# Mixer B's values product in three rounded parts, with small operations moved to GpSimd

## The chip, the cores and the metric

The kernel runs on one core of one Trainium2 chip. A core has five engines that run their own instruction queues in order: TensorE (PE, matmuls and transposes into PSUM), VectorE (DVE), ScalarE (ACT), GpSimd (POOL) and SyncE (SP, which issues transfers). The metric is the device time of one execution, in microseconds; of several runs the median is told. A profiled execution gives the trace, from which the rows below come.

## The reference

A two-layer encoder trunk over 512 positions of width 1024, all in fp32. Layer 0 has a dilated window attention (mixer A), layer 1 a latent attention (mixer B); each is followed by a squared-ReLU MLP. What matters here is mixer B:

```python
lat = h @ w_in                                   # 256 q latents, 128 kv latents, 64 rotary key
q  = (rms_norm(c_q, q_a_gain) @ w_qb)            # 8 heads x (128 + 64)
kv = (rms_norm(c_kv, kv_a_gain) @ w_kvb)         # 8 heads x (128 keys + 128 values)
q, k = rms_norm(q, q_gain), rms_norm(k, k_gain)  # k = key part and the shared rotary key
# rope on the last 64 of q and k
p = softmax(q k^T / sqrt(192)); o = p v          # every position attends to every position
return o @ w_o
```

## The kernel before

The kernel is written as a program that a scheduler turns into one queue for each engine: it lists operations in program order and picks, by its own cost model, which ready operation goes next on its engine. So an edit in one place can move instructions of the same stretch on every engine. Tiles come from pools with a fixed number of buffers; a new tile in a used buffer waits for the last reader of the old one.

Almost all matmuls work on rounded parts: a value x is split into `hi` (x in the reduced fp32 format F32R, written by ScalarE) and `lo` (x - hi, written by VectorE), and a product is the sum of hi*hi, hi*lo and lo*hi. One product of mixer B is not: probabilities times values (`pv_b`, L1157) reads plain fp32 tiles.

Mixer B works as follows. The latents of four row blocks are projected (L1162) and normalised (`evac_lat`, L996): squares are summed on ScalarE, epsilon is added on VectorE, the power -0.5 is taken on GpSimd (both in `rstd_of`, L127), and VectorE scales. The rotary key is made by three products on VectorE and a sum on GpSimd. Heads go in four pairs. For a pair, `kv_chunk` projects one row block of keys and values (L1051), scales the keys (`ks`, L1105) and transposes them; `q_chunk` does the same for queries, with their rotary part in three products on VectorE (L1069, L1072) and a sum on GpSimd (L1076). Their PSUM tiles come from a pool of two banks.

Scores come next, one block of 128 queries of one head per step (`score`, L1125): five matmuls (L1133), the row maximum on VectorE (L1135), its product with the query's scale on VectorE (L1136), the exponential on ScalarE (L1138), the reciprocal of the sum (L1139) and the normalisation (L1140) on VectorE. Three steps later the block is transposed by TensorE and copied out of PSUM, even blocks by VectorE (L1151), odd ones by ScalarE (L1149). After the fourth block of a head comes the product with the values, `pv_b`, whose result is split into parts for the output projection (L1159, L1160). In the first three pairs scores, transposed blocks and outputs share a pool of four PSUM banks; in the last pair these four hold the output projection, whose matmuls run beside the scores.

The chunks of the next pair are laid between the steps by a table, `plan`: from the third step of a pair on, one or two chunks a step; the first two steps of a pair have none of the next pair. Weight blocks of the projections behind are also split in this stretch (L158 on ScalarE, L159 on VectorE).

Of the kernel before, what the change touches and what calls it, by code (L numbers as in the profile page):

```python
# [10 lines left out]
F32 = mybir.dt.float32  # L11
# [77 lines left out]
def encoder_kernel(ctx: ExitStack, tc: tile.TileContext, x, norm_mix, norm_ffn, a_w_qkv, a_q_gain, a_k_gain,  # L89
# [37 lines left out]
    def rstd_of(ss, n, add, name, out=None):  # L127

        v = st.tile([P, 8], F32, tag="rs_v", name=nm("rs_v"))
        V.tensor_scalar(v[:, :n], ss, add, None, op0=ALU.add)  # L130
        if out is None:
            out = st.tile([P, 8], F32, tag=name, name=nm(name))[:, :n]
        G.tensor_tensor(out, v[:, :n], nhalf[:, :n], op=ALU.pow)  # L133
        return out
# [835 lines left out]
    if True:  # L970
        with tc.tile_pool(name="bpool", bufs=1, reuse_waits="tile") as bp, \
# [10 lines left out]
            cgB = bp.tile([P, NT, 2, RD], F32, name="cgB")  # L982
            sgB = bp.tile([P, NT, 2, RD], F32, name="sgB")

            with tc.issue_after(marks["sum"]):
                for t in range(2):
                    for hf in range(2):
                        gb = gr[:, t, hf * 32:hf * 32 + 32].unsqueeze(1).broadcast_to([P, NT, 32])
                        G.tensor_tensor(cgB[:, :, t, hf * 32:hf * 32 + 32], cosB, gb, op=ALU.mult)
                        G.tensor_tensor(sgB[:, :, t, hf * 32:hf * 32 + 32], sinB, gb, op=ALU.mult)  # L990
                G.tensor_scalar(sgB[:, :, :, 32:64], sgB[:, :, :, 32:64], -1.0, None, op0=ALU.mult)
# [4 lines left out]
            def evac_lat(r, acc):  # L996
# [6 lines left out]
                rs = rstd_of(ss[:, 0:2], 2, EPS, "lrs")  # L1003
                cn = bw.tile([P, QL + KVL], F32, tag="cn", name=nm("cn"))
# [3 lines left out]
                t2 = bw.tile([P, 2 * RD], F32, tag="kr2", name=nm("kr2"), bufs=1)[:, 0:RD]  # L1008
# [17 lines left out]
            def new_pair(p):  # L1026
# [4 lines left out]
                d["v"] = bw.tile([P, NT, 2, DH], F32, tag="vb", name=nm("vb"), bufs=2)  # L1031
# [23 lines left out]
            def q_chunk(d, r):  # L1055
# [8 lines left out]
                rstd_of(ss[:, 0:2], 2, QKD * EPS, None, d["rq"][:, r])  # L1064
                qs = bw.tile([P, 2, DH], F32, tag="qs", name=nm("qs"), bufs=2)
                A.activation(qs, a3[:, :, 0:DH], AF.Copy)
                rt = bw.tile([P, 2, RD], F32, tag="rt", name=nm("rt"), bufs=1)
                r2 = bw.tile([P, 2, RD], F32, tag="r2", name=nm("r2"), bufs=1)
                V.tensor_tensor(rt, a3[:, :, DH:QKD], cgB[:, r, 0].unsqueeze(1).broadcast_to([P, 2, RD]), op=ALU.mult)  # L1069
# [176 lines left out]
```

## Time and profile before

| | |
|---|---|
| median of 3 runs | 1409.34 us (1408.19 to 1409.35) |
| the profiled execution | 1411.71 us, of which the span of the trace 1409.9 us |
| granted TensorE clock, mean | 0.999 |
| TensorE busy | 1374.4 us, 97% |
| VectorE busy | 940.8 us, 67% |
| ScalarE busy | 801.2 us, 57% |
| GpSimd busy | 225.3 us, 16% |

Shares are averages over stages with different limits. Matmuls are pipelined, so the busy time of one contains waiting; the distance from one matmul's start to the next tells more. The chain of waits follows the work that ended last back through the engines. An idle time in the timeline has, behind an arrow, what ended it.

### The profile page before, as it was taken

The numbers are of one execution on the slowest core, as the hardware profiler recorded it, in microseconds if no ns is written. First come the engines' busy times: TensorE is split into PE (matmuls) and PEld (weight loads), VectorE is DVE, ScalarE is ACT, GpSimd is POOL, SyncE is SP. The second block draws the span as 40 slices with busy tenths as digits, with TensorE's granted clock in tenths as the row PEclk, the third lists the DMA queues.
The fourth block names the chain that finished last, engine by engine and source line by source line (L and its number), as shares of the span: only waits on it lengthen the run. The fifth ranks groups of instructions, "written<-read, shape, count | busy, mean of one in ns | idle before, by whom it ended". The sixth has DMA issues, their size and how long they took to land.

```text
span 1409.9 us, 18981 instructions
## 1 busy us (share of the span) xinstructions
PE 1374.4 (97%) x6852; PEld 1165.1 (83%) x6852; DVE 940.8 (67%) x1498; ACT 801.2 (57%) x1643; POOL 225.3 (16%) x240
## 2 busy tenths in 40 slices
PE   7999999999999999999999999899999999999998
PEld 6999878888889979888888878776768888888886
DVE  6885777787788744574655768788644465574747
ACT  6544778687786624553536455777523553644543
POOL 1110212121122001020200204523101020020201
PEclk9999999999999999999999999999999999999999
DMA  9535554655555538586683934200114758493835
GB/s 304 167 134 160 134 133 98 164 130 126 143 131 119 155 105 244 159 187 172 124 234 91 234 90 94 60 30 31 45 45 165 194 125 233 92 236 121 197 87 120
DMA packets 171774, 197.83 MB, mean 140 GB/s; under 512 B 59104, under 2 KB 109024, under 8 KB 171680
## 3 DMA queue, kind: packets, MB, share of 16 engines
q1 hardware_dynamic: 152496, 157.55, 37.8%
q0 software_dynamic: 19184, 39.07, 15.4%
q8 instruction: 54, 0.88, 0.3%
q14 instruction: 40, 0.33, 0.1%
HBM read 176.13 MB, written 7.86 MB: 130 GB/s over the span
## 4 chain that ended last, share of the span: by engine, by line
PE 80%; DVE 7%; DMA 5%; ACT 5%; issue 2%; SPq 0%; POOL 0%; ACTq 0%; DVEq 0%; POOLq 0%
PE acc L183 45%; PE sc L860 11%; PE tp L860 7%; DMA xT<-t 3%; PE tp L125 3%; PE sc L422 2%; PE acc L1157 1%; PE sc L1051 1%; PE acc L1133 1%; PE tp L422 1%; DVE wlo L803 1%; PE acc L422 1%; PE sco L702 1%; ACT junk L138 1%; PE sc L588 1%
## 5 line engine op out<-in xcount | busy, mean ns | idle before, releaser
L183 PE MATMUL acc<-whi,hT 128*128 128x512 f32 (+2 forms) x1208 | 378.0, 389 | 1.9 <-ACT hT L744 1.0
L183 PE MATMUL acc<-hT_f,whi 128*128 128x512 f32 (+1 forms) x1152 | 316.6, 366 | 0.0
L159 DVE TENSOR_TENSOR wlo<-raw,whi 128x1024 fp32r<-128x1024 f32 (+3 forms) x146 | 173.1, 1189 | 162.4 <-ACT whi L158 161.8
L183 PEld LDWEIGHTS acc<-whi,hT 128*128 128x128 f32 x1208 | 225.0, 189 | 43.5 <-ACT hT L744 1.8
L158 ACT ACTIVATE whi<-raw 128x1024 fp32r<-128x1024 f32 (+3 forms) x146 | 149.9, 1029 | 160.6 <-PE acc L183 64.4
L183 PEld LDWEIGHTS acc<-hT_f,whi 128*128 128x128 f32 x1152 | 207.5, 189 | 34.7
L183 PE MATMUL acc<-wlo,hT 128*128 128x512 f32 (+2 forms) x604 | 233.5, 387 | 0.7 <-DVE wlo L159 0.7
L803 DVE TENSOR_TENSOR wlo<-wqs,whi 128x1024 fp32r<-128x1024 f32 x112 | 137.7, 1232 | 112.4 <-ACT whi L802 112.2
L802 ACT ACTIVATE whi<-wqs 128x1024 fp32r<-128x1024 f32 x112 | 118.3, 1060 | 160.5 <-PE acc L183 66.2
L183 PE MATMUL acc<-hT_f,wlo 128*128 128x512 f32 (+1 forms) x576 | 204.1, 365 | 0.0
L860 PE MATMUL sc<-whi,asp 128*128 128x512 f32 x512 | 165.0, 389 | 1.2 <-DVE resid L834 1.2
L788 POOL DMA_DIRECT2D wqs<-in_ffn_w_dram x64 | 77.6, 1344 | 536.8 <-DVE wlo L803 356.5
L183 PEld LDWEIGHTS acc<-wlo,hT 128*128 128x128 f32 x604 | 113.8, 189 | 20.4 <-DVE wlo L159 1.1
L183 PEld LDWEIGHTS acc<-hT_f,wlo 128*128 128x128 f32 x576 | 108.2, 189 | 17.5
L860 PEld LDWEIGHTS sc<-whi,asp 128*128 128x128 f32 x512 | 96.1, 188 | 21.8 <-issue 2.0
L860 PE MATMUL tp<-whi,asp 128*128 128x512 f32 x352 | 112.1, 389 | 0.9 <-DVE resid L834 0.9
L133 POOL TENSOR_TENSOR qrs<-rs_v,nhalf 128x4 f32<-128x4 f32 x48 | 65.9, 1375 | 264.6 <-DVE rs_v L130 233.7
L860 PE MATMUL sc<-wlo,asp 128*128 128x512 f32 x256 | 99.6, 389 | 0.0
L296 ACT ACTIVATE qkT<-xT 128x1024 uint16<-128x1024 uint16 x48 | 56.5, 1183 | 43.0 <-DMA xT<-t 42.8
L860 PEld LDWEIGHTS tp<-whi,asp 128*128 128x128 f32 x352 | 66.1, 188 | 15.0 <-DVE resid L834 1.3
L860 PE MATMUL tp<-wlo,asp 128*128 128x512 f32 x176 | 68.1, 389 | 0.0
L138 ACT ACTIVATE junk<-acc 128x128 f32<-128x128 f32 x192 | 52.2, 272 | 11.0 <-PE acc L183 7.3
(236 smaller groups left out, 2189.0 us busy)
## 6 DMA issues: line engine op xcount, KB each, us to landing
wqs<-in_ffn_w_dram SPq DMA_DIRECT2D x80, 512.0 KB, 5.6
raw<-in_ffn_w_dram SPq DMA_DIRECT2D x64, 512.0 KB, 4.4
wqs<-in_ffn_w_dram POOLq DMA_DIRECT2D x64, 512.0 KB, 7.9
raw<-in_a_w_qkv_dram SPq DMA_DIRECT2D x96, 256.0 KB, 3.2
b<-in_a_w_qkv_dram SPq DMA_DIRECT2D x24, 384.0 KB, 5.7
vall<-vo POOLq DMA_DIRECT2D x24, 192.0 KB, 2.3
raw<-in_a_w_o_dram SPq DMA_DIRECT2D x8, 512.0 KB, 4.2
raw<-in_b_w_o_dram SPq DMA_DIRECT2D x8, 512.0 KB, 3.8
```

Source lines behind the costliest of these rows:

```text
L125: return PE.transpose(o, i, ident)
L133: G.tensor_tensor(out, v[:, :n], nhalf[:, :n], op=ALU.pow)
L138: A.activation(junk, x, AF.Square, scale=1.0 / math.sqrt(dim), accum_out=out)
L158: A.activation(hi[:, :nk, :n], raw[:, :nk, :n], AF.Copy)
L159: V.tensor_tensor(lo[:, :nk, :n], raw[:, :nk, :n], hi[:, :nk, :n].bitcast(F32), op=ALU.subtract)
L183: PE.matmul(accs[o][:, oc], lhsT=lt, rhs=rt, start=(kt == 0 and p_i == 0 and hv == 0), stop=(kt == total - 1 and p_i == 2), skip_group_che ...
L296: A.activation(dst, xT.rearrange("p (h c) t -> p c t h", h=2), AF.Copy)
L422: PE.matmul(banks[t][:, :VH], lhsT=lt, rhs=rt[:, j], start=(first and k == 0 and i_ == 0), stop=(k == 3 and i_ == 2), skip_group_check=True)
L788: marks["sum"] = nc.gpsimd.dma_start(t, src, accum_op=ALU.add).ins
L802: A.activation(hi, x, AF.Copy)
L803: V.tensor_tensor(lo, x, hi.bitcast(F32), op=ALU.subtract)
L860: PE.matmul(bk[t], lhsT=lt, rhs=rt[:, j], start=(first and k == 0 and i_ == 0), stop=(k == 3 and i_ == 2), skip_group_check=True)
```

## The change

The product of probabilities and values is made of three products of rounded parts, like the others. The values get a rounded part and a remainder (`vl`, VectorE; for odd pairs in the buffer of the gain table), the transposed probabilities too: all 32 blocks are rounded by ScalarE, and VectorE writes all 32 remainders. One tile of parts serves all heads; before, two heads had a tile each. The sum with epsilon in the reciprocal roots of mixer B, and the scaling of a maximum, go from VectorE to GpSimd. The rotary products of a query chunk are one operation on VectorE instead of three, from a table `csB` in which cosines and sines stand together, and the sum on GpSimd is two operations; likewise for the rotary key. The normalised latents take a buffer of the probabilities' tag.

```diff
-    def rstd_of(ss, n, add, name, out=None):
+    def rstd_of(ss, n, add, name, out=None, on=None):
...
-        V.tensor_scalar(v[:, :n], ss, add, None, op0=ALU.add)
+        (on or V).tensor_scalar(v[:, :n], ss, add, None, op0=ALU.add)
...
-                V.tensor_tensor(krr[:, r], acc[:, 384:448], cgB[:, r, 1], op=ALU.mult)
-                V.tensor_tensor(t2[:, 0:32], acc[:, 416:448], sgB[:, r, 1, 32:64], op=ALU.mult)
-                V.tensor_tensor(t2[:, 32:64], acc[:, 384:416], sgB[:, r, 1, 0:32], op=ALU.mult)
-                G.tensor_tensor(krr[:, r], krr[:, r], t2, op=ALU.add)
+                V.tensor_tensor(t2, acc[:, 384:448].unsqueeze(1).broadcast_to([P, 2, RD]), csB[:, r, 1], op=ALU.mult)
+                for hf in range(2):
+                    o_ = 32 - 32 * hf
+                    G.tensor_tensor(krr[:, r, hf * 32:hf * 32 + 32], t2[:, 0, hf * 32:hf * 32 + 32],
+                                    t2[:, 1, o_:o_ + 32], op=ALU.add)
...
-                d["v"] = bw.tile([P, NT, 2, DH], F32, tag="vb", name=nm("vb"), bufs=2)
+                d["v"] = [bw.tile([P, NT, 2, DH], F32R, tag="vb", name=nm("vb"), bufs=2),
+                          gp.tile([P, NT, 2, DH], F32R, tag="gain", name=nm("vl")) if p % 2 else
+                          bw.tile([P, NT, 2, DH], F32R, tag="vl", name=nm("vl"), bufs=1)]
...
-                V.tensor_tensor(rt, a3[:, :, DH:QKD], cgB[:, r, 0].unsqueeze(1).broadcast_to([P, 2, RD]), op=ALU.mult)
+                V.tensor_tensor(rt, a3[:, :, DH:QKD].unsqueeze(1).broadcast_to([P, 2, 2, RD]),
+                                csB[:, r, 0].unsqueeze(2).broadcast_to([P, 2, 2, RD]), op=ALU.mult)
...
-                rs = rstd_of(ss[:, 0:2], 2, ssr[:, r:r + 1], "krs")
-                A.activation(d["v"][:, r], a4[:, :, 1], AF.Copy)
+                rs = rstd_of(ss[:, 0:2], 2, ssr[:, r:r + 1], "krs", on=G)
+                vh, vl = (t[:, r] for t in d["v"])
+                A.activation(vh, a4[:, :, 1], AF.Copy)
+                V.tensor_tensor(vl, a4[:, :, 1], vh.bitcast(F32), op=ALU.subtract)
...
-                V.tensor_scalar(mx[:, 1:2], mx[:, 0:1], rq, -1.0, op0=ALU.mult, op1=ALU.mult)
+                G.tensor_scalar(mx[:, 1:2], mx[:, 0:1], rq, -1.0, op0=ALU.mult, op1=ALU.mult)
...
-                    dst = pT[:, :, r * P:(r + 1) * P]
-                    if r % 2:
-                        A.activation(dst, tv, AF.Copy)
-                    else:
-                        V.tensor_copy(dst, tv)
+                    hi, lo = (pT[:, c, :, r * P:(r + 1) * P] for c in range(2))
+                    A.activation(hi, tv, AF.Copy)
+                    V.tensor_tensor(lo, tv, hi.bitcast(F32), op=ALU.subtract)
...
-                    PE.matmul(o, lhsT=d["v"][:, j, h], rhs=pT[:, j], start=(j == 0), stop=(j == NT - 1))
+                    vh, vl = (t[:, j, h] for t in d["v"])
+                    for i, (lt, c) in enumerate(((vh, 0), (vh, 1), (vl, 0))):
+                        PE.matmul(o, lhsT=lt, rhs=pT[:, c, j], start=(j == 0 and i == 0), stop=(j == NT - 1 and i == 2))
```

The scheduler orders the new operations anew, from the first latent on; three places show it. Line numbers of the new file differ by up to three (the values product L1157 is L1160, a score's maximum L1135 is L1138).

On TensorE, the product of the third head (first head of the second pair) in the kernel before, between a query projection (L1051) and scores (L1133):

```order
L125 MATMUL acc_8892<-ck,pe_8687 128x128 x4
L1051 MATMUL sc_8776<-whi_8657,cT 128x384
L1051 MATMUL sc_8776<-wlo_8658,cT 128x384
L1051 MATMUL sc_8776<-whi_8657,cT 128x384 x2
L1051 MATMUL sc_8776<-wlo_8658,cT 128x384
L1051 MATMUL sc_8776<-whi_8657,cT 128x384
L1157 MATMUL acc_8898<-pTs,vb_8192 128x512 x4
L1133 MATMUL acc_8939<-kn_8190,qn_8565 128x512 x3
```

and in the changed kernel the end of it, whose first matmul stands eighteen rows ahead:

```order
L1053 MATMUL sc_8931<-whi_8671,cT 128x384
L125 MATMUL acc_8976<-ck,pe_8767 128x128 x3
L1160 MATMUL acc_8916<-pT,vb_8186 128x512
L1160 MATMUL acc_8916<-pT,vl_8187 128x512
L1160 MATMUL acc_8916<-pT,vb_8186 128x512 x2
L1160 MATMUL acc_8916<-pT,vl_8187 128x512
L1160 MATMUL acc_8916<-pT,vb_8186 128x512 x2
L1160 MATMUL acc_8916<-pT,vl_8187 128x512
L1160 MATMUL acc_8916<-pT,vb_8186 128x512 x2
L1160 MATMUL acc_8916<-pT,vl_8187 128x512
L125 MATMUL acc_8976<-ck,pe_8767 128x128
```

One matmul of the twelve needs only the rounded part; a score block and two query projections stand between it and the other eleven.

On VectorE, the same change of pairs before. `ks_8727` is the key scaling of a chunk, `wlo_9633` the remainder of a weight of the output projection:

```order
L1140 TENSOR_SCALAR pe_8749<-pe_8749,bmx_8746 128x512
L130 TENSOR_SCALAR rs_v_8722<-kss_8719,ssr 128x2
L1135 TENSOR_REDUCE bmx_8823<-acc_8817 128x1
L1151 COPY pTs<-acc_8830 128x4x128
L1136 TENSOR_SCALAR bmx_8823<-bmx_8823,rqs_76 128x1
L159 TENSOR_TENSOR wlo_9633<-raw_9630,whi_9632 128x1024
L1105 TENSOR_TENSOR ks_8727<-sc_8714,krs_8724 128x256
L1119 SCALAR_TENSOR_TENSOR kn_8646<-tp_8799,gn,kn_8646 128x2x128
```

and after (`ks_8745` and `wlo_9712` are the same two operations, `vl_8662` the value remainder of that chunk):

```order
L1152 TENSOR_TENSOR pT<-acc_8706,pT 128x4x128
L1138 TENSOR_REDUCE bmx_8764<-acc_8758 128x1
L1142 RECIPROCAL bmx_8699<-bmx_8699 128x1
L1143 TENSOR_SCALAR pe_8702<-pe_8702,bmx_8699 128x512
L1106 TENSOR_TENSOR vl_8662<-sc_8731,vb_8661 128x256
L1122 SCALAR_TENSOR_TENSOR kn_8659<-tp_8749,gn,kn_8659 128x2x128
L1108 TENSOR_TENSOR ks_8745<-sc_8731,krs_8741 128x256
L159 TENSOR_TENSOR wlo_9712<-raw_9709,whi_9711 128x1024
L1138 TENSOR_REDUCE bmx_8841<-acc_8835 128x1
```

The key scaling stands ahead of the weight's remainder now, and a value remainder ahead of the key scaling.

On GpSimd, the same stretch before holds powers (L133) and key products (L1107) alone:

```order
L133 TENSOR_TENSOR krs_8671<-rs_v_8669,nhalf 128x2
L1107 TENSOR_TENSOR kd_8676<-krr,krs_8671 128x256
L133 TENSOR_TENSOR krs_8707<-rs_v_8705,nhalf 128x2
L1107 TENSOR_TENSOR kd_8712<-krr,krs_8707 128x256
L133 TENSOR_TENSOR krs_8724<-rs_v_8722,nhalf 128x2
L1107 TENSOR_TENSOR kd_8729<-krr,krs_8724 128x256
L133 TENSOR_TENSOR krs_8769<-rs_v_8767,nhalf 128x2
L1107 TENSOR_TENSOR kd_8774<-krr,krs_8769 128x256
```

and after (`bmx` are the maxima's scalings, `rs_v` the sums):

```order
L1139 TENSOR_SCALAR bmx_8699<-bmx_8699,rqs_76 128x1
L130 TENSOR_SCALAR rs_v_8739<-kss_8736,ssr 128x2
L1139 TENSOR_SCALAR bmx_8764<-bmx_8764,rqs_76 128x1
L133 TENSOR_TENSOR krs_8741<-rs_v_8739,nhalf 128x2
L1110 TENSOR_TENSOR kd_8747<-krr,krs_8741 128x256
L1139 TENSOR_SCALAR bmx_8841<-bmx_8841,rqs_76 128x1
L130 TENSOR_SCALAR rs_v_8786<-kss_8783,ssr 128x2
L133 TENSOR_TENSOR krs_8788<-rs_v_8786,nhalf 128x2
L1110 TENSOR_TENSOR kd_8794<-krr,krs_8788 128x256
```

A maximum's scaling now stands behind a power and a key product in one queue.

## Rows read from the trace of the kernel before

**Rows 1.** Windows, three stretches of mixer B: stretch, length, busy time (instructions) per engine, clock, DMA

```profile
883.00:920.00 37.00, 32.49 (x173) 26.61 (x172) 31.09 (x101) 30.20 (x119) 18.59 (x30) 1.00 0.19 57
...
927.00:1003.00 76.00, 72.88 (x359) 53.85 (x358) 64.96 (x183) 54.68 (x179) 24.97 (x36) 1.00 0.09 28
1003.00:1049.00 46.00, 44.52 (x201) 33.45 (x200) 24.93 (x55) 17.49 (x34) 0.82 (x2) 1.00 0.16 46
```

**Rows 2.** Chain of waits: start us, us, the engine and line it runs through

```profile
941.04 3.43 PE acc L1157 x8
944.47 1.16 PE acc L1133 x5
...
1040.28 3.71 PE tp L1157 x8
```

**Rows 3.** Timeline of TensorE: start us, us, instruction, [idle before <-releaser]

```profile
954.34 0.41 PE L1051 MATMUL sc<-whi,cT 128*128 128x384 f32 x1 [1.23 <-DVE ks L1105]
...
987.27 0.41 PE L1051 MATMUL sc<-whi,cT 128*128 128x384 f32 x1 [1.22 <-DVE ks L1105]
```

**Rows 4.** Timeline of VectorE around that wait

```profile
952.53 1.33 DVE L159 TENSOR_TENSOR wlo<-raw,whi 128x1024 fp32r<-128x1024 f32 x1
953.78 0.41 DVE L1105 TENSOR_TENSOR ks<-sc,krs 128x256 f32<-128x256 f32 x1
```

**Rows 5.** Groups on VectorE, mixer B: busy us, mean ns of one, idle before

```profile
L1140 DVE TENSOR_SCALAR pe<-pe,bmx 128x512 f32<-128x512 f32 x32 | 16.9, 531 | 0.8
...
L1151 DVE COPY pTs<-acc 128x512 f32<-128x512 f32 x12 | 8.2, 680 | 0.0
...
L1136 DVE TENSOR_SCALAR bmx<-bmx,rqs 128x1 f32<-128x1 f32 x32 | 6.5, 207 | 0.3
L1072 DVE TENSOR_TENSOR r<-sc,sgB 128x64 f32<-128x64 f32 x32 | 5.6, 214 | 0.0
...
L1105 DVE TENSOR_TENSOR ks<-sc,krs 128x256 f32<-128x256 f32 x12 | 5.0, 415 | 0.0
L1069 DVE TENSOR_TENSOR rt<-sc,cgB 128x128 f32<-128x128 f32 x16 | 4.6, 286 | 1.6 <-ACT qs L1066 1.4
L130 DVE TENSOR_SCALAR rs_v<-kss,ssr 128x2 f32<-128x2 f32 x16 | 4.2, 262 | 0.1
L1160 DVE TENSOR_TENSOR hT<-acc,hT 128x512 fp32r<-128x512 f32 x6 | 4.2, 692 | 3.5 <-ACT hT L1159 3.5
```

**Rows 6.** Groups on GpSimd, mixer B

```profile
L1076 POOL TENSOR_TENSOR rd<-rt,r 128x256 f32<-128x256 f32 x16 | 11.7, 734 | 5.1 <-DVE r L1072 2.3 <-DVE rs_v L130 2.2 <-DVE bmx L1139 0.3
L133 POOL TENSOR_TENSOR krs<-rs_v,nhalf 128x2 f32<-128x2 f32 x16 | 11.5, 722 | 36.4 <-DVE rs_v L130 36.1
...
L1107 POOL TENSOR_TENSOR kd<-krr,krs 128x256 f32<-128x256 f32 x16 | 9.8, 614 | 1.0
...
L1012 POOL TENSOR_TENSOR krr<-krr,kr 128x64 f32<-128x64 f32 x4 | 1.3, 320 | 2.9 <-DVE kr L1011 2.7 <-DVE ssr L1002 0.3
```

**Rows 7.** Groups on ScalarE, mixer B

```profile
L1149 ACT ACTIVATE pTs<-acc 128x512 f32<-128x512 f32 x12 | 7.3, 605 | 4.1 <-PE acc L125 4.1
```

**Rows 8.** Timeline of TensorE in the first stretch

```profile
902.30 1.29 PE L1051 MATMUL sc<-w,cT 128*128 128x384 f32 x6 [0.88 <-DVE r L1072]
```

**Rows 9.** Timeline of VectorE, two normalisations of a score block

```profile
956.08 0.47 DVE L1140 TENSOR_SCALAR pe<-pe,bmx 128x512 f32<-128x512 f32 x1
...
957.85 1.05 DVE L1140 TENSOR_SCALAR pe<-pe,bmx 128x512 f32<-128x512 f32 x1
```

**Rows 10.** Timeline of GpSimd at the second of them

```profile
957.90 0.72 POOL L1076 TENSOR_TENSOR rd<-rt,r 128x256 f32<-128x256 f32 x1
```

**Rows 11.** SyncE's issue of the norm gain, timeline

```profile
895.60 0.34 SPq L233 DMA_DIRECT2D g_ffn<-in_norm_ffn_dram  x1
```

**Rows 12.** Timeline of TensorE behind mixer B

```profile
1061.02 1.07 PE L125 MATMUL tp<-ck,xn 128*128 128x128 f32 x8 [2.07 <-DVE xn L216]
```

**Rows 13.** Windows, a stretch behind mixer B

```profile
1062.00:1065.00 3.00, 3.00 (x9) 2.33 (x9) 2.21 (x3) 0.77 (x2) 0.00 (x0) 0.51 0.03 5
```

More of the change, by code (lines that the diff above doesn't have):

```diff
@@ L981, in encoder_kernel @@
                 nc.sync.dma_start(gn[:, t:t + 1], src[0, 0:DH].unsqueeze(1))
-            cgB = bp.tile([P, NT, 2, RD], F32, name="cgB")
-            sgB = bp.tile([P, NT, 2, RD], F32, name="sgB")
+            csB = bp.tile([P, NT, 2, 2, RD], F32, name="csB")
             with tc.issue_after(marks["sum"]):
@@ L1002, in evac_lat @@
                 V.tensor_scalar(ssr[:, r:r + 1], ssr[:, r:r + 1], EPS, None, op0=ALU.add)
-                rs = rstd_of(ss[:, 0:2], 2, EPS, "lrs")
-                cn = bw.tile([P, QL + KVL], F32, tag="cn", name=nm("cn"))
+                rs = rstd_of(ss[:, 0:2], 2, EPS, "lrs", on=G)
+                cn = bw.tile([P, S], F32, tag="pe", name=nm("cn"), bufs=3)
                 V.scalar_tensor_tensor(cn[:, 0:QL], acc[:, 0:QL], rs[:, 0:1], gl[:, 0:QL], op0=ALU.mult, op1=ALU.mult)
@@ L1007, in evac_lat @@
                                        op1=ALU.mult)
-                t2 = bw.tile([P, 2 * RD], F32, tag="kr2", name=nm("kr2"), bufs=1)[:, 0:RD]
-                V.tensor_tensor(krr[:, r], acc[:, 384:448], cgB[:, r, 1], op=ALU.mult)
-                V.tensor_tensor(t2[:, 0:32], acc[:, 416:448], sgB[:, r, 1, 32:64], op=ALU.mult)
-                V.tensor_tensor(t2[:, 32:64], acc[:, 384:416], sgB[:, r, 1, 0:32], op=ALU.mult)
-                G.tensor_tensor(krr[:, r], krr[:, r], t2, op=ALU.add)
+                t2 = bw.tile([P, 2, RD], F32, tag="kr2", name=nm("kr2"), bufs=1)
+                V.tensor_tensor(t2, acc[:, 384:448].unsqueeze(1).broadcast_to([P, 2, RD]), csB[:, r, 1], op=ALU.mult)
[3 more added lines that the diff above has]
+                                    t2[:, 1, o_:o_ + 32], op=ALU.add)
                 tp = tp_p.tile([P, 512], F32, tag="tp", name=nm("tp"))
@@ L1062, in q_chunk @@
                     A.activation(junk[:, 0:QKD], a3[:, h], AF.Square, accum_out=ss[:, h:h + 1])
[L1064 removed]
+                rstd_of(ss[:, 0:2], 2, QKD * EPS, None, d["rq"][:, r], on=G)
                 qs = bw.tile([P, 2, DH], F32, tag="qs", name=nm("qs"), bufs=2)
                 A.activation(qs, a3[:, :, 0:DH], AF.Copy)
[L1067 to L1069 removed]
+                rt = bw.tile([P, 2, 2, RD], F32, tag="rt", name=nm("rt"), bufs=1)
+                V.tensor_tensor(rt, a3[:, :, DH:QKD].unsqueeze(1).broadcast_to([P, 2, 2, RD]),
+                                csB[:, r, 0].unsqueeze(2).broadcast_to([P, 2, 2, RD]), op=ALU.mult)
+                rd = bw.tile([P, 2, 2, RD], F32, tag="rd", name=nm("rd"), bufs=2)
                 for hf in range(2):
                     o_ = 32 - 32 * hf
[L1072 to L1077 removed]
+                    G.tensor_tensor(rd[:, :, :, hf * 32:hf * 32 + 32],
+                                    rt[:, 0, :, hf * 32:hf * 32 + 32].unsqueeze(2).broadcast_to([P, 2, 2, 32]),
+                                    rt[:, 1, :, o_:o_ + 32].unsqueeze(2).broadcast_to([P, 2, 2, 32]), op=ALU.add)
                 def part2():
@@ L1176, in encoder_kernel @@
             lag = 3
-            pend, tail, nxt, pT, pTs = [], [], None, None, None
+            pend, tail, nxt, pT = [], [], None, None
             plan = {2: [(kv_chunk, 0)], 3: [(kv_chunk, 1), (kv_chunk, 2)], 4: [(kv_chunk, 3), (q_chunk, 0)],
@@ L1188, in encoder_kernel @@
                     if r2 == 0:
-                        if pTs is None:
-                            pTs = x16.tile([P, 2, NT, S], F32, tag="x16", name="pTs")
-                        pT = pTs[:, h2]
+                        if pT is None:
+                            pT = x16.tile([P, 2, NT, S], F32R, tag="x16", name="pT")
                     f(pT)
```

11 lines of the change are left out of this document (3 added, 8 removed).

## The prediction

> **What bounds the kernel now.** I read the page's table by engine first: TensorE is busy in 97% of the span, so a microsecond counts only if it is taken from TensorE's row or from a wait in it. Everything that the diff touches lies in mixer B, some 166 of the 1409.9 us, so the next view is the busy time by stretch [rows 1]. Three stretches differ. In the first, 37 us in which the latents, the first keys and the first queries are made, ScalarE and VectorE are busy for 30.2 and 31.1 us and TensorE waits in between. In the second, 76 us of three head pairs, TensorE is busy for 72.9 us, but VectorE has 65.0 and ScalarE 54.7: TensorE leads, VectorE is close. In the third, 46 us, matmuls of the output projection fill TensorE's row and VectorE has 24.9 us of work; here TensorE alone sets the pace.
>
> The chain of waits shows what one product of probabilities and values costs [rows 2]: eight passes (four full-fp32 matmuls in two passes each) take 3.43 us, and the five three-part score matmuls behind them 1.16 us, 0.232 us for each 512 columns. Then come the waits. The timeline of TensorE has two alike in the second stretch, 1.23 and 1.22 us, on a key chunk's scaling on VectorE [rows 3]; VectorE's own timeline shows why: that scaling (ks) stands in the queue behind the 1.33 us split of an output weight [rows 4].
>
> **The change part by part.** *The product itself.* Twelve matmuls of rounded parts replace eight passes: 12 x 0.232 = 2.78 us against 3.43 [rows 2], 0.65 us less a head, 5.2 us for eight heads if nothing else were late. How much stays, head by head: the first two heads stand where the timeline of TensorE shows no idle time, and the sixth and seventh have projection matmuls beside them; these four I take in full, -2.6 us. The three heads in between stand beside VectorE's waits; half, -1.0 us. The last head has no other work in front of it. It starts when the last transposed block is out of PSUM (the 3.71 us at 1040.28 in [rows 2]); the rounded part now comes from ScalarE and the remainder after it from VectorE, about 0.69 us (a subtraction of the same shape, L1160 in [rows 5]). The first of the twelve needs no remainder and covers 0.23 of that, so this head saves 0.65 - 0.46 = 0.2 us. Sum -3.8, bounds -5.2 and 0.
>
> *The remainders on VectorE.* Sixteen of the 32 transposed blocks were copied there at 0.680 us and now all 32 are subtracted at about 0.692; the 32 scalings of the maximum at 0.207 leave; sixteen value remainders of 256 elements come, which I price like the key scaling of that shape, 0.415; the query's rotary part is one operation of 256 elements (0.415 again) instead of 0.286 + 2 x 0.214 = 0.714; 36 small sums of up to 0.262 leave [rows 5]. Per head pair: off 4 x 0.680 + 8 x 0.207 + 4 x 0.714 + 8 x 0.262 = 9.3, on 8 x 0.692 + 4 x 0.415 + 4 x 0.415 = 8.9 us. VectorE's load hardly moves, but its place does. At a change of pairs no query or key chunk fills TensorE, and a step is a score block and a transposed block: there VectorE loses 0.207 and half a copy, 0.34, and gains 0.692, so each step is 0.14 longer. Four steps at three changes give 1.7 us, of which I take half, since TensorE leads again soon after: +0.9. At the same place the value remainders of two chunks stand in front of the next maximum (0.83 a change, 2.5 in all, where the key chunks' small sums leave about half): I take a quarter, +0.6. The remainder's tile of one buffer makes its first write wait for the product two pairs earlier, and behind it in VectorE's queue stand two key scalings and the next maximum; but in the kernel before the output's remainder, which waits for the same product and for ScalarE besides, stood there, so this wait costs nothing more. Sum +1.5, bounds 0 and +4.2.
>
> *The order around the two long waits.* In the new order the key scaling stands in front of the weight's split, not behind it. The 1.23 and 1.22 us of [rows 3] lose their cause; next late is the value remainder, put in front of the scaling (0.415), and the wait for its GpSimd power. I take -1.5 of -2.4, bounds -2.4 and 0.
>
> *GpSimd.* It gets 36 sums of 128x2, 32 scalings of 128x1 and the rotary sums in two halves. The trace has no such small sum or scaling on it; the nearest row is a sum of 128x64 at 0.320, the highest a power of 128x2 at 0.722 (which holds far more than a sum) [rows 6]. From 0.320 for 64 elements and 0.614 for 256 a line leads to 0.22 at none, and I take 0.22 for each. A split rotary sum costs one such start more, 0.734 to 0.96. Per pair that is 16 x 0.22 + 4 x 0.22 = 4.4 us on an engine busy for 25.0 of 76 [rows 1]: it has room. What counts is the chain. A reciprocal root loses a hop: its sum runs on the engine of its power. A maximum gains one, and ScalarE's exponential waits for it; three steps lie between a score and its use, so I price it at nothing while GpSimd's queue is short, and as a rival below when it is not.
>
> ScalarE takes sixteen more evacuations at 0.605 [rows 7], 2.4 us a pair on 54.7 of 76; PSUM banks of the transposed blocks stay taken some 0.6 longer. Room hides both, at nothing, bounds 0 and +1.
>
> *The first stretch.* VectorE loses twelve small sums of up to 0.262 there and 0.3 us of each of four query and four key rotary products, and gains four value remainders, 0.415 each: some 3 us less. A projection waited 0.88 us for exactly these rotary products to leave the bank [rows 8]. GpSimd gains six small sums, a split key sum and a split query sum, about 2 us, in a run of powers that leads to the last key block. Opposite and alike in size: 0, bounds -1.5 and +2.
>
> *Contention.* A normalisation of a score block on VectorE takes 0.47 us, but 1.05 when it starts beside a rotary sum on GpSimd, and ends soon after it [rows 9, 10]; the mean of 32 is 0.531 [rows 5], 0.06 above the undisturbed one. I take no more of it than now. The Trainium skill (GPSIMD Engine Reference, section "8. Key points") says that GpSimd shares its SBUF interfaces with VectorE and names contention with VectorE's two-port modes. By that rule the excess grows with GpSimd's busy time, from 25 to some 38 us in the second stretch, 0.06 to 0.09 each, 1 us on VectorE, and with half of it showing the sum would be -3.3 instead of -3.8. The one row agrees with the rule.
>
> *The norm gain.* The value remainder of odd pairs lives in the gain's tile. The gain was loaded at 895.6 [rows 11]; now its load waits for the last product and stands on SyncE's queue between the second and the third weight block of the next MLP. Its user is the first normalisation behind mixer B, and the next blocks wait for free buffers in any case: nothing.
>
> Sum: -3.8 + 1.5 - 1.5 + 0 = -3.8 us. The profiled execution ran 1411.7 (span 1409.9), so it would be 1407.9; it lies 2.4 us above the median of the runs, 1409.3, from which the same step gives **1405.5**.
>
> **The rivals.** *VectorE takes it back* (within 0.2%). If VectorE paces the whole second stretch, only the sixth to eighth heads save, 1.5 us, and the waits of [rows 3] move to the remainders: 1409.3 - 1.5 = 1407.8. For it: 65.0 busy of 76 us. Against: no idle TensorE at the first pair.
>
> *The scaling waits on GpSimd* (slower). GpSimd works in order; a maximum's scaling now queues behind a power or a key product, 0.722 or 0.614 us [rows 6]. In the twelve steps at the changes of pairs there are but four banks for scores and transposed blocks, so a late exponential holds TensorE. With 0.6 us each, 12 x 0.6 = 7.2, less the 3.8: +3.4, 1412.7. It decides from 0.32 us a step. Against it: the scaling on VectorE queued as well, behind a copy of 0.68. The Trainium skill (GPSIMD Engine Reference, section "4.1 Engine selection") puts elementwise work on VectorE and calls GpSimd about twice as slow with two inputs; by that, the scaling itself would take 0.41 instead of 0.207, 2.5 us more over these steps, and this rival would end at 1415.2. The trace agrees in part: sums or products of 64 elements take 0.320 on GpSimd and 0.214 on VectorE [rows 5, 6].
>
> *Everything falls away* (more). All heads in full, both waits, the first stretch shorter: -5.2 - 2.4 - 1.5 = -9.1, 1400.2.
>
> *The products are no cheaper.* If rounded parts ran like full fp32, twelve would cost more than four, 10.3 us a head against 3.43, and the time would be some 55 us longer; the score products, of the same parts, run at 0.232 and speak against it.
>
> The clock can shift any case. Behind mixer B TensorE waits 2.07 us for a normalisation [rows 12], and just after it the granted clock is 0.51 for some 3 us [rows 13], the lower of its two levels, 1.2 GHz; at that level half of those 3 us, some 1.5, is lost. If it stays up there, or falls once more elsewhere, the time moves by that either way.
>
> **How the numbers follow.** The forecast 0.48, its own range 1402.5 to 1407.5; VectorE takes it back 0.27; the scaling waits 0.17; everything falls away 0.06; no cheaper 0.02. A difference of 0.2% (2.8 us) is about what a measurement tells from none, so the border lies at 1406.5. A fifth of the forecast lies above it, and 0.02 of the scaling's case ends within it: faster 0.38 + 0.06 = 0.44, the same 0.10 + 0.27 + 0.02 = 0.39, slower 0.15 + 0.02 = 0.17. The range 1401.5 to 1411.5 leaves out the far ends of the first and of the slower rival.
>
> **What would show it.** In the new profile twelve matmuls of L1160 a head at 0.23 us apart; in the chain some 2.8 us a head; no wait of 1.2 us on ks. VectorE takes it back: waits of TensorE on L1152 or L1106. The scaling waits: ScalarE idle until GpSimd's L1139, and TensorE until the exponential L1141. I am wrong if the stretch from the first latent to the last product shortens by under 2 us, or if the time changes outside it.

## The result, and the profile after

The changed kernel takes 1413.15 us (median of 8 runs, 1411.26 to 1415.31) against 1409.34 (8 runs, 1408.19 to 1411.98): a ratio of 1.0028, 95% interval 1.0019 to 1.0037. It is slower by some 3.8 us; the forecast was faster by 3.8. The profiled execution, the slowest of the eight, took 1415.31 us (span 1413.5).

Behind mixer B nothing changed. The wait of [rows 12] is there again, 3.55 us later, and from it to the end of the trace it is 348.9 us in both kernels:

```profile
1064.57 1.46 PE L125 MATMUL tp<-ck,xn 128*128 128x128 f32 x8 [2.07 <-DVE xn L216]
```

Ahead of mixer B this execution was 0.8 us earlier: TensorE transposes the first latent at 888.98 instead of 889.77 (over the profiles of all runs this point lies between 886.9 and 889.8). So mixer B itself takes 4.3 us longer in this profile. The windows, in the order of [rows 1], then a stretch inside mixer B and the one that answers to [rows 13] (stretch, length, busy time and instructions of PE, PEld, DVE, ACT and POOL, clock, DMA share, GB/s):

```profile
883.00:920.00 37.00, 33.88 (x179) 27.23 (x178) 29.78 (x76) 31.29 (x125) 28.13 (x61) 1.00 0.19 58
926.00:1006.00 80.00, 72.06 (x382) 58.43 (x381) 67.16 (x148) 60.68 (x192) 39.15 (x85) 0.98 0.10 28
1006.00:1052.60 46.60, 44.70 (x213) 35.85 (x212) 25.84 (x49) 18.09 (x35) 2.40 (x8) 1.00 0.17 55
942.50:945.50 3.00, 3.00 (x8) 2.31 (x7) 0.67 (x3) 0.00 (x0) 0.00 (x0) 0.50 0.00 0
1065.00:1068.00 3.00, 3.00 (x12) 2.52 (x11) 2.48 (x3) 1.19 (x2) 0.23 (x1) 0.52 0.03 5
```

The first window has the same length by choice. That this stretch lost nothing is seen elsewhere: the last block of the first head is transposed 35.4 us after the first latent (924.39), against 35.9 (925.70). The loss is in the second stretch, which takes 80 us instead of 76, and with less work in it: all but one matmul of the sixth head's product now stand behind it, in the third, which is 0.6 us longer. The fourth row is new: for 3 us the clock is granted at half, and VectorE and ScalarE do next to nothing.

The chain shows the product in the first three heads, to be set against [rows 2] (eleven of twelve matmuls stand together):

```profile
928.84 2.54 PE acc L1160 x11
942.74 3.93 PE acc L1160 x11
962.66 2.56 PE acc L1160 x11
```

At full clock a matmul takes 0.231 us and twelve 2.77, as forecast; the second head ran at half clock, some 1.4 us more. So a matmul costs what it should. What took the gain back is in TensorE's waits in mixer B (engine, line waited for, us in total, times, longest):

```profile
PE acc L1160 <- ACT pT L1151: 1.9, 3, 1.0
PE sc L1136 <- DVE rt L1070: 1.6, 1, 1.6
PE acc L125 <- DVE pT L1152: 1.4, 3, 0.5
PE acc L1136 <- ACT pe L1141: 1.3, 1, 1.3
PE sc L1053 <- DVE rt L1070: 1.2, 1, 1.2
```

The two waits of [rows 3] are gone from the second stretch. In their place TensorE waits nine times in mixer B for the evacuation of a transposed block, in either part (4.8 us in all, the last head's included; before, once, 0.7), and once for an exponential. The longest wait, 1.6 us, is like those of [rows 3]: at the end of the second stretch a score waits for a rotary product (`rt`) which stands in VectorE's queue behind a weight's split (VectorE's split, its rotary product, TensorE's score):

```profile
1003.03 1.23 DVE L159 TENSOR_TENSOR wlo<-raw,whi 128x1024 fp32r<-128x1024 f32 x1 [0.74 <-ACT whi L158]
...
1004.57 0.41 DVE L1070 TENSOR_TENSOR rt<-sc,csB 128x256 f32<-128x256 f32 x1
```

```profile
1005.12 0.93 PE L1136 MATMUL sc<-kn,qn 128*128 128x512 f32 x3 [1.62 <-DVE rt L1070]
```

The timelines of ScalarE, VectorE and TensorE show where the waits for transposed blocks begin (start, us, instruction, idle time before it and what ended it):

```profile
946.47 0.66 ACT L1105 ACTIVATE vb<-sc 128x256 fp32r<-128x256 f32 x2 [4.18 <-PE acc L1160]
```

```profile
946.89 0.42 DVE L1106 TENSOR_TENSOR vl<-sc,vb 128x256 fp32r<-128x256 f32 x1 [3.69 <-ACT vb L1105]
```

```profile
939.81 0.49 PE L1160 MATMUL acc<-pT,vb 128*128 128x512 f32 x1 [0.23 <-ACT pT L1151]
941.58 1.16 PE L1136 MATMUL acc<-kn,qn 128*128 128x512 f32 x3 [1.27 <-ACT pe L1141]
942.54 0.63 PE L1160 MATMUL acc<-pT,vb 128*128 128x512 f32 x1
942.96 0.63 PE L1160 MATMUL acc<-pT,vl 128*128 128x512 f32 x1
...
956.00 0.63 PE L125 MATMUL acc<-ck,pe 128*128 128x128 f32 x4 [0.53 <-DVE pT L1152]
...
958.12 0.50 PE L1160 MATMUL acc<-pT,vb 128*128 128x512 f32 x1 [1.05 <-ACT pT L1151]
```

Read from the top: at 946.47 ScalarE copies out the third pair's first values. Their tile has two buffers, so it is the first pair's, and it is free only when that pair's second product has ended. For 4.18 us ScalarE has this copy at the head of its queue, and VectorE behind it the values' remainder for 3.69. The product itself is late: its first matmul waits 0.23 us for a transposed block, a score that stands between it and the other eleven 1.27 us for an exponential, and after that idle time the matmuls stand 0.42 us apart (the half clock). From 947 on both engines catch up, and while they do TensorE waits for transposed blocks (956.00, 958.12). In the kernel before the same copy stands behind the copy of that product's output, which waits 0.16 us for the product, and starts at 945.0:

```profile
944.51 0.60 ACT L1159 ACTIVATE hT<-acc 128x512 fp32r<-128x512 f32 x1 [0.16 <-PE acc L1157]
945.00 0.66 ACT L1103 ACTIVATE vb<-sc 128x256 f32<-128x256 f32 x2
```

Durations, to be set against [rows 5 to 7] (busy us, mean ns of one, idle before; VectorE, ScalarE, GpSimd):

```profile
L1152 DVE TENSOR_TENSOR pT<-acc,pT 128x512 fp32r<-128x512 f32 x24 | 16.2, 680 | 0.5 <-ACT pT L1151 0.4
L1143 DVE TENSOR_SCALAR pe<-pe,bmx 128x512 f32<-128x512 f32 x32 | 15.8, 494 | 0.9
```

```profile
L1151 ACT ACTIVATE pT<-acc 128x512 fp32r<-128x512 f32 x24 | 15.0, 631 | 0.7 <-PE acc L125 0.6
```

```profile
L1076 POOL TENSOR_TENSOR rd<-rt 128x128 f32<-128x128 f32 x32 | 14.3, 469 | 5.9 <-DVE rt L1070 4.5 <-DVE bmx L1142 1.2
...
L1139 POOL TENSOR_SCALAR bmx<-bmx,rqs 128x1 f32<-128x1 f32 x32 | 9.2, 287 | 53.6 <-DVE bmx L1138 52.0 <-DVE bmx L1142 1.3
L130 POOL TENSOR_SCALAR rs_v<-qss 128x2 f32<-128x2 f32 x16 | 5.3, 332 | 9.6 <-ACT junkb L1064 8.9
```

### The profile page after: what moved, and what is told of

Its sections match the earlier page's. It is cut to its first block, busy times and chain, and to the rows that moved or that the text cites. A ratio compares the mean times of both kernels' runs of the same rounds, so it can differ in the third digit from the quotient of the medians.

```text
span 1413.5 us, 19072 instructions
## 1 busy us (share of the span) xinstructions
PE 1373.5 (97%) x6884; PEld 1172.4 (83%) x6884; DVE 941.6 (67%) x1422; ACT 808.7 (57%) x1659; POOL 250.2 (18%) x328
## 4 chain that ended last, share of the span: by engine, by line
PE 78%; DVE 7%; ACT 6%; DMA 5%; issue 3%; POOL 1%; SPq 0%; ACTq 0%; DVEq 0%
PE acc L183 44%; PE sc L860 11%; PE tp L860 7%; DMA xT<-t 3%; PE tp L125 2%; PE sc L422 2%; PE acc L1160 1%; PE acc L1136 1%; PE tp L422 1%; DVE wlo L803 1%; PE acc L422 1%; ACT t L288 1%; PE sc L1053 1%; PE sco L702 1%; ACT whi L158 1%
## 5 line engine op out<-in xcount | busy, mean ns | idle before, releaser
L133 POOL TENSOR_TENSOR qrs<-rs_v,nhalf 128x4 f32<-128x4 f32 x48 | 65.9, 1376 | 264.3 <-DVE rs_v L130 233.3
```

## The experiments

Every edit makes the scheduler order mixer B anew, so single edits are read in pairs. Ratios are to the kernel before on the same chip; they are taken over all runs and can differ by 0.1% from the quotient of two medians.

**First round: which part of the change loses?** Theory A: the evacuation in series, in which a transposed block leaves PSUM by ScalarE's rounding and then by VectorE's subtraction. Theory B: the moves to GpSimd.

```diff
-                G.tensor_scalar(mx[:, 1:2], mx[:, 0:1], rq, -1.0, ...)
+                V.tensor_scalar(mx[:, 1:2], mx[:, 0:1], rq, -1.0, ...)
```

> The changed kernel with one edit: the scaling of the maximum runs on VectorE again. Theory A (evacuation in series: a transposed block now leaves PSUM by ScalarE's rounded part and then VectorE's remainder, 0.63 + 0.68 us instead of one copy of 0.60 or 0.68, and the product and the next blocks wait for it): the loss stays, 1412 to 1415 us. Theory B (small operations on GpSimd: the scaling waits in its queue, the exponential comes late and holds a score's bank): most of the 1.27 us wait on the exponential and the low clock behind it go, and all of the scaling's price with them: 1406 to 1409.

Measured 1416.66 us, ratio 1.0052 (1.0040 to 1.0065): slower still, and above A's range too. The scaling on GpSimd is a gain here, and B falls in its main point.

```diff
-                rstd_of(..., on=G)        # three places, and the scaling as above
+                rstd_of(...)
```

> The changed kernel with the scaling and the small sums of the reciprocal roots on VectorE again; the product in three parts and the rotary product as one stay. Theory A: the product alone carries the loss, 1412 to 1416 us. Theory B: without the moves to GpSimd the predicted gain appears, 1404 to 1408.

Measured 1411.73 us, 1.0020 (1.0011 to 1.0029): the product loses without the moves too, just under A's range.

```diff
-                    A.activation(hi, tv, AF.Copy)
-                    V.tensor_tensor(lo, tv, hi.bitcast(F32), op=ALU.subtract)
+                    (one copy, ScalarE for odd r, VectorE for even)
...
-                    for i, (lt, c) in enumerate(((vh, 0), (vh, 1), (vl, 0))):
+                    PE.matmul(o, lhsT=d["v"][:, j, h], rhs=pT[:, j], ...)
```

> The changed kernel with the product in full fp32 again (no remainders, one copy a transposed block, by ScalarE and VectorE in turn); small sums and scaling on GpSimd and the rotary product as one stay. Theory A: no loss without the product, 1406 to 1410 us. Theory B: the loss without the product's gain, 1411 to 1417.

As in the kernel before, the values have one plain tile and two heads a tile of probabilities each. Measured 1407.48 us, 0.9989 (0.9980 to 0.9997): as A has it. The rest of the change is a small gain.

The kernel before with the rotary products' diff and the latents' new buffer alone:

> The kernel before with the rotary products as one alone (VectorE has some 0.3 us less for each of 16 query chunks and 0.2 for four key chunks). Both theories: 1407 to 1410 us. Outside that range the order that the scheduler picks anew would itself be worth microseconds, and neither theory could be read from single edits.

Measured 1409.30 us, 1.0005 (0.9996 to 1.0014): nothing. So the product costs +0.15% without the moves (1.0005 to 1.0020) and +0.39% beside them (0.9989 to 1.0028).

**Second round: what in the product?** Theory C came from the trace: the wait of the third pair's values for the first pair's product.

```diff
                     A.activation(hi, tv, AF.Copy)
-                    V.tensor_tensor(lo, tv, hi.bitcast(F32), op=ALU.subtract)
...
-                        PE.matmul(o, lhsT=lt, rhs=pT[:, c, j], ...)
+                        PE.matmul(o, lhsT=lt, rhs=pT[:, 0, j], ...)
```

> The changed kernel without the 32 remainders of the probabilities on VectorE; the product reads the rounded part in their place, so TensorE's twelve matmuls a head stay. It leaves out the remainder's share of the product. Theory A (evacuation in series): a transposed block leaves PSUM by one operation again and VectorE has 22 us less, so the loss and more goes: 1405 to 1409 us. Theory C (in the trace of the changed kernel ScalarE stands 4.18 us and VectorE 3.69 us before the values of the third pair, whose tile waits for a product of the first pair; what is late from there makes TensorE wait): little changes, 1411 to 1414.

Measured 1403.75 us, 0.9954 (0.9941 to 0.9967): more than A has, and not what C has.

```diff
-                d["v"] = [bw.tile(..., tag="vb", bufs=2),
-                          gp.tile(..., tag="gain") if p % 2 else bw.tile(..., tag="vl", bufs=1)]
+                d["v"] = [oB[:, 6 + i].rearrange(...) for i in range(2)] if p == 2 else \
+                         [bw.tile(..., tag="vb", bufs=2),
+                          gp.tile(..., tag="gain") if p == 1 else bw.tile(..., tag="vl", bufs=1)]
```

> The changed kernel with the third pair's values and their remainders in two slots of the output's tile that are written only by the last two heads, so that no value chunk waits for a product of an earlier pair. Theory C: the waits of 4.18 and 3.69 us go, and 2 to 4 us with them, 1409 to 1411.5 us. Theory A: ScalarE then waits as long at the output behind it in its queue, and the time stays, 1412 to 1414.5.

Measured 1403.42 us, 0.9954 (0.9941 to 0.9966): 0.74% below the changed kernel (1.0028), more than C expected, with every remainder still made. It leaves nothing out and beats both kernels. TensorE's largest waits in mixer B there:

```profile
PE sc L1054 <- DVE rt L1071: 1.2, 1, 1.2
PE acc L183 <- ACT hT L1163: 0.9, 2, 0.7
PE tp L125 <- DVE ks L1109: 0.9, 2, 0.6
PE acc L1161 <- DVE pT L1153: 0.8, 2, 0.4
PE tp L1161 <- ACT pT L1152: 0.8, 1, 0.8
```

The scheduler lays the third pair's value chunks earlier now: the first values leave PSUM at 933.26 (the tile is named by its slot), 13 us sooner, and the work spreads. Two windows of the kernel before, of the changed kernel and of this one (columns as above):

```profile
940.00:950.00 10.00, 10.00 (x48) 7.00 (x47) 8.87 (x24) 6.18 (x17) 1.69 (x3) 1.00 0.00 0
950.00:960.00 10.00, 8.77 (x37) 5.95 (x36) 8.69 (x25) 7.46 (x25) 4.07 (x6) 1.00 0.17 55
```

```profile
940.00:950.00 10.00, 8.72 (x35) 6.81 (x35) 6.18 (x15) 4.13 (x12) 1.16 (x4) 0.83 0.00 0
950.00:960.00 10.00, 8.40 (x48) 6.76 (x47) 9.59 (x23) 9.19 (x30) 6.00 (x13) 1.00 0.19 55
```

```profile
933.26 0.39 ACT L1106 ACTIVATE hT<-sc 128x256 fp32r<-128x256 f32 x1
```

```profile
940.00:950.00 10.00, 9.58 (x52) 7.97 (x52) 9.55 (x22) 7.80 (x24) 5.53 (x12) 1.00 0.19 55
950.00:960.00 10.00, 10.00 (x59) 8.94 (x58) 9.75 (x23) 9.22 (x32) 5.66 (x12) 1.00 0.00 0
```

In the changed kernel VectorE (the third busy time) falls to 6.18 of 10 us and is then full at 9.59 with TensorE waiting; here it is nearly full in both windows (9.55 and 9.75), and TensorE is too.

```diff
                     A.activation(hi, tv, AF.Copy)
-                    V.tensor_tensor(lo, tv, hi.bitcast(F32), op=ALU.subtract)
+                    V.tensor_tensor(lo, hi.bitcast(F32), hi.bitcast(F32), op=ALU.subtract)
...                                     (and the product reads pT[:, 0, j], as above)
```

> The changed kernel with the 32 probabilities' remainders still made on VectorE, but from the rounded part in SBUF alone (a subtraction of the same shape that does not read PSUM), and with the product reading the rounded part in their place. VectorE's load stays about as it is, the bank is free after ScalarE, and no product waits for a remainder. It leaves out the remainder's share of the product. Theory A by its two halves: if the load of VectorE is what costs, 1411 to 1414 us, as the changed kernel; if the bank held twice as long and the product's wait for the remainder cost, 1405 to 1409, as without remainders.

Measured 1407.71 us, 0.9982 (0.9973 to 0.9991): most of the fifth experiment's gain, though VectorE's operation takes 0.725 us here against 0.680:

```profile
L1152 DVE TENSOR_TENSOR pT<-pT 128x512 fp32r<-128x512 f32 x32 | 23.1, 725 | 3.2 <-ACT pT L1151 3.1
```

So VectorE's load is kept, and a bank held shorter and a product that doesn't wait for the remainder are worth 0.46% of the 0.74% that the fifth experiment gave back.

```diff
-                V.tensor_tensor(vl, a4[:, :, 1], vh.bitcast(F32), op=ALU.subtract)
...
-                    for i, (lt, c) in enumerate(((vh, 0), (vh, 1), (vl, 0))):
+                    for i, (lt, c) in enumerate(((vh, 0), (vh, 1), (vh, 0))):
```

> The changed kernel without the 16 remainders of the values on VectorE (0.417 us each, 6.7 us in all); the third matmul reads the rounded values in their place. It leaves out that share of the product. Theory A: the values' remainders matter little beside the probabilities', 1411 to 1413 us. If VectorE's load alone set the time, a third of the gain of leaving out the probabilities' 22 us would show: 1409 to 1411.

Measured 1410.19 us, 0.9997 (0.9989 to 1.0006): 6.7 us less on VectorE are worth 0.31%, as the reading by VectorE's load had it. These three kernels leave out a part of the product. In their traces no engine stands idle before a value chunk for a product, though the buffers are as in the changed kernel: with the evacuation shorter or VectorE freer, the product ends in time. Counted from the first transposed latent, the last matmul of the second head's product starts at 54.1 us in the kernel before, at 57.3 in the changed one, and at 52.0, 52.8 and 53.1 in these three. In the sixth experiment's kernel it starts at 55.4, late again, but no value waits for it. So A and C are read as two halves of one loop: a product made late by its evacuations holds up the values, and the values hold up the evacuations behind them.

**Third round: is it that wait, and which tile's?**

The third experiment's kernel with `bufs=3` for the value tile:

> The kernel with full-fp32 products, one copy a transposed block, small operations on GpSimd and the rotary product as one (the third experiment), with a third buffer for the value tile, so that no value chunk waits for a product there either. Theory C as the runs now have it (the wait of the third pair's values for a product of the first pair is harmless beside short evacuations, and costs some 10 us beside the product in parts): 1406 to 1409 us, as without the buffer. The other reading (free values are worth as much in any kernel, and the product in parts still costs what it did): 1397 to 1401.

Measured 1406.84 us, 0.9982 (0.9973 to 0.9991), against 0.9989 without the buffer: beside the full-fp32 product the wait is harmless within the noise.

Only the rounded values of the third pair in a free slot:

> The changed kernel with only the third pair's rounded values in a free slot of the output's tile; their remainders keep the tile that the first pair used, and wait for its product. If the remainder's tile of one buffer holds the loss (VectorE waits at its first write, and the key scaling and the next maximum behind it), 1411 to 1414 us. If ScalarE's wait at the rounded values holds it, 1403 to 1406.

Measured 1412.69 us, 1.0024 (1.0015 to 1.0034); now VectorE waits 2.7 us in two at the remainder. Only the remainders in a free slot:

> The changed kernel with only the third pair's value remainders in a free slot; the rounded values keep their two buffers, as in the kernel before, and wait for the first pair's product. If the remainder's tile of one buffer holds the loss, 1403 to 1406 us. If ScalarE's wait holds it, or either of the two is enough, 1411 to 1414.

Measured 1412.86 us, 1.0029 (1.0018 to 1.0041). Either wait alone is enough for the loss. The waits at the values in the changed kernel and in these two (us in total, times, longest):

```profile
ACT vb L1105 <- PE acc L1160: 5.0, 2, 4.2
```

```profile
DVE vl L1107 <- PE acc L1161: 2.7, 2, 1.9
```

```profile
ACT vb L1106 <- PE acc L1161: 3.4, 2, 2.6
```

These two profiles have no half clock there, and the longest wait is 1.9 and 2.6 us instead of 4.2 with about the same loss: some 1.6 us of the 4.2 came with the half clock.

The sixth experiment's kernel with scaling and sums on VectorE:

> The fastest kernel so far (product in parts, values that wait for nothing) with the small sums and the scaling of the maximum on VectorE again. If the moves to GpSimd are worth something only by VectorE's load, which is near its limit in this stretch, 1405 to 1409 us, slower than 1403.4. If they are worth nothing here, 1402 to 1404.5.

Measured 1405.02 us, 0.9973 (0.9964 to 0.9981): the moves to GpSimd are worth 0.19% there.

**Fourth round: why is the wait dear only beside the product in parts?** D1: VectorE is too full to make up for any standing. D2: the single tile of probabilities.

```diff
+                        pT = oB[:, 4:8].rearrange(...) if h2 and d["p"] < 2 else pT0
```

> The changed kernel with a second tile of probabilities for heads 1 and 3 (four slots of the output's tile that the fifth and later heads write), so that the transposed blocks of the next head need not wait for a product; the third pair's values still wait. D2 (the single tile makes the wait costly): 1403.5 to 1407 us. D1 (VectorE is too full to make up for any standing): 1410 to 1413.5.

Measured 1411.95 us, 1.0023 (1.0013 to 1.0032): D2 falls. The score's wait for an exponential inside the second product is as long in this profile and in those of the tenth and eleventh experiments as in the changed kernel's (in that order):

```profile
940.47 0.96 PE L1136 MATMUL acc<-kn,qn 128*128 128x512 f32 x3 [1.28 <-ACT pe L1141]
```

```profile
941.13 0.96 PE L1137 MATMUL acc<-kn,qn 128*128 128x512 f32 x3 [1.27 <-ACT pe L1142]
```

```profile
941.99 0.97 PE L1137 MATMUL acc<-kn,qn 128*128 128x512 f32 x3 [1.26 <-ACT pe L1142]
```

The fifth to eighth experiments' profiles have no such wait there.

```diff
-                d["v"] = bw.tile(..., tag="vb", bufs=2)
+                d["v"] = gp.tile(..., tag="gain") if p == 1 else bw.tile(..., tag="vb", bufs=2)
```

> The kernel before (full-fp32 product, small operations on VectorE, rotary products in parts) with the second pair's values in the norm gain's tile, so that the third and fourth pairs' values take buffers that are long free. D1: VectorE is as full in the kernel before (125.2 of 161.6 us), so free values are worth some 3 to 6 us there too, 1403 to 1406.5. D2: two tiles of probabilities give the engines work during the product, and the wait costs nothing there: 1408 to 1410.

Measured 1407.63 us, 0.9983 (0.9975 to 0.9992): the wait costs the kernel before some 2.4 us too, less than D1 expected and more than D2. So D1 is what is left, but no run shows it by itself.

> The fastest kernel so far (product in parts, free values; 1403.4 us) with the scaling of the maximum alone back on VectorE, 0.207 us there against 0.287 on GpSimd. If the scaling's place in GpSimd's queue costs something, 1401 to 1403; if VectorE's 6.6 us of it cost more, 1404.5 to 1407; if neither shows, between them.

Measured 1407.82 us, 0.9994 (0.9985 to 1.0004), 0.8 us past the range for VectorE's load: the scaling on GpSimd is worth 0.40% here, as it was worth 0.24% in the first experiment. The sums alone go the other way (0.9973 with both on VectorE, 0.9994 with the sums on GpSimd; 1.0020 and 1.0052 with the waits). Why the sums lose without the scaling is not settled: each of these kernels has an order of its own.

What free values (values whose tiles wait for no product) are worth, from five pairs that differ in little else; each difference is uncertain by some 0.09 to 0.16%, so the 0.07% can't be told from nothing:

| kernel | values wait | values free | difference |
|---|---|---|---|
| before | 1 | 0.9983 | 0.17% |
| full-fp32 product, sums and scaling on GpSimd | 0.9989 | 0.9982 | 0.07% |
| product in parts, all small operations on VectorE | 1.0020 | 0.9973 | 0.47% |
| product in parts, scaling on VectorE | 1.0052 | 0.9994 | 0.58% |
| the changed kernel | 1.0028 | 0.9954 | 0.74% |

## Why the prediction was wrong, point by point

**The product itself** (-3.8, bounds -5.2 and 0) was right in its price: it runs at 0.231 us a matmul. What it brings can only be measured together with its remainders, for which the prediction added 1.5, so -2.3 for both. Where nothing waits, both bring 0.28% or 3.9 us beside the moves to GpSimd (0.9982 to 0.9954; adding the two intervals in squares, 1.8 to 6.1), but only 0.10% or 1.4 us, not clear of nothing, with the small operations on VectorE (0.9983 to 0.9973; these two differ in the rotary products too, which were worth nothing by themselves).

**The remainders on VectorE** is the step that failed, in its last sentences: "The remainder's tile of one buffer makes its first write wait for the product two pairs earlier", and at the end "so this wait costs nothing more". It saw the wait and set it against the one that stood there before, the output's remainder. It asked what the waiting instruction delays, but took the product's own end as given. The product now ends later against the work around it: its last matmul starts 57.3 us after the first transposed latent instead of 54.1, and still at 55.6 to 56.0 in the three profiles with about the same loss and no half clock. Two operations of 0.63 and 0.68 us in series stand before it where one stood, and a score inside it waits for an exponential; how much of the delay each of these, and VectorE's load, makes is not told apart. While the product is late, ScalarE and VectorE stand together at the head of their queues, in a stretch where VectorE is full; that this is what makes each microsecond dear is argued from the windows. It also named one tile alone: the rounded values' two buffers, untouched in number, wait for the same product, and either is enough (tenth and eleventh experiments). Free values make 0.74%, 10.4 us, of the changed kernel and 0.17%, 2.4 us, of the kernel before: the wait costs some 8 us more than it did, where the step put nothing. The step's upper bound was +4.2; the whole miss, from 1405.5 to 1413.15, is 7.6.

**ScalarE's evacuations and the banks**, "at nothing, bounds 0 and +1", failed with it: taking the remainder off PSUM and out of the product's way alone gave back 0.46%, 6.5 us. That price holds beside the waiting values; with free values it was not measured, but TensorE waits for transposed blocks only some 2.2 us in all there.

**The order around the two long waits** was right for these two: both are gone. It did not see that another of the same kind would come, the 1.62 us behind a weight's split at 1005.12. The kernel with the rotary products alone keeps both waits (1.21 and 1.20 us) and the time; the third experiment's has neither and is 0.16%, 2.2 us, below it, but has the small operations moved as well, so the 1.5 us for them can't be told apart.

**The first stretch**, 0, was right: the last block of the first head comes 0.5 us sooner after the first latent, with GpSimd busy for 28.1 of 37 us. The norm gain's load, too, cost nothing that the waits behind mixer B show.

**GpSimd's durations**: the scaling takes 0.287 and the sums 0.332 or less, against an estimate of 0.22; the two halves of a split rotary sum 14.3 / 16 = 0.89 us of GpSimd, against 0.96. The hop that a maximum's scaling gained, priced at nothing, shows no loss: with the scaling on GpSimd the kernel is faster, twice. So the rival that ended slower, the scaling that waits on GpSimd, named the wrong mechanism for the right side, and that its 1412.7 lies 0.5 us from the measured time is luck. One wait like it is there (TensorE's 1.27 us before 941.58: the scaling in front of that exponential stood 0.5 us behind a key product), but the second experiment's kernel, with the scaling on VectorE, waits for an exponential there too, 1.06 us.

**VectorE takes it back** came closest in mechanism: waits on L1152 appeared, as it said. It allowed for the loss of the gain, though not for more, because it counted VectorE's busy time, not the time in which VectorE must stand. The prediction's own sign of being wrong came true as well: from the first transposed latent to the last product's last matmul it was 153.6 us and is 158.1.

**Contention.** With GpSimd busy for 39 of 80 us the normalisation's mean fell from 0.531 to 0.494, so no growth with GpSimd's busy time shows here. Single ones are still longer beside a rotary sum: one takes 0.72 at 959.68, with such sums on GpSimd from 959.24 to 960.12. The Trainium skill (GPSIMD Engine Reference, "8. Key points") names this contention; that its excess grows with GpSimd's busy time was the prediction's reading, and the trace does not agree with that.

**The place of small operations.** One scaling is shorter on VectorE (0.207 against 0.287), and yet its place on GpSimd gained 0.24% and 0.40%; that VectorE was the nearly full engine is the likely reason. The Trainium skill (GPSIMD Engine Reference, "4.1 Engine selection") puts elementwise work on VectorE, but gives its factor of two for operations with two inputs and calls one input roughly line-rate. The scaling is an operation with one input and a scalar for each partition, so the 0.41 that the rival worked out did not follow from it.

**The clock** fell once more, as the text allowed, after the idle time at 940 to 942; at 0.50 for 3 us it cost some 1.4 us of the profiled run. It isn't the cause: among the eight runs those at a mean clock of 1.000 took 1411.3 and 1412.5 us, where the kernel before at 1.000 took 1408.5 to 1409.2 (its medians on four chips).

## What to carry to other kernels

When a product is made cheaper by operations in front of it, look for everything that waits for its end, above all tiles with few buffers whose next writer stands at the head of an engine's queue: a wait that cost 1 to 2 us beside a short chain cost 7 to 10 beside a longer one here. Before giving up such a change, look for dead space for those tiles (here two slots of the output that are written last): the same change then was 6.5 us faster than the kernel before. Price an engine that is nearly full by the time in which it must stand, not by its sum of work.

## What the runs showed of the hardware that was not expected

TensorE's clock, 2.4 GHz, went to half, 1.2, after idle times of 1.27 and 2.07 us in this kernel's profile, for some 3 us each; the profiles of several experiments, the fastest among them, show no such fall after 883 us up to 1070. So the idle time does not decide it alone: the tenth, eleventh and thirteenth profiles have the wait of 1.26 to 1.28 us at the same place, and the fastest kernel's the 2.07 us behind mixer B, at full clock. What decides it is not shown. ScalarE's evacuation of a transposed block took 0.631 us in the mean in the changed kernel (0.605 before), and the exponential 0.809 where it took 0.784. It is not the rounded format: the same evacuation takes 0.606 in the sixth experiment's kernel. The cause is not shown.
